# A hybrid decoder layer on one core: the second half's second FFN product in four accumulation steps, two of them by block products

## The chip, the cores and the metric

The program runs on one core of a Trainium2 chip. Times are device microseconds of one execution (us). The core's engines are TensorE (PE in the profile, its weight loads PEld), VectorE (DVE), ScalarE (ACT), GpSimd (POOL) and SyncE (SP). Each executes its own list of instructions in order. Transfers are issued by SyncE, GpSimd and (at the very end) ScalarE, and carried by 16 transfer engines that they share.

## What is computed

One layer, weights shared by a prompt (1 x 1024 tokens) and a sample group (8 x 4 tokens), model width 1024, FFN width 2816:

```python
h = _rmsnorm(x, norm1_g) * (1.0 + sc1) + sh1       # sh, sc, gt from silu(c) @ ada_w + ada_b
u = h @ w_in                                       # inputs of both branches and of the gates
y_a = h_lru * gelu(u_g)                            # causal convolution, RG-LRU
y_b = o * silu(u_r)                                # chunked GLA, head norm
m = sigmoid(u_ga) * (y_a @ proj_a) + sigmoid(u_gb) * (y_b @ proj_b)
x = x + gt1 * (m @ w_out)
h2 = _rmsnorm(x, norm2_g) * (1.0 + sc2) + sh2
f1, f2 = jnp.split(h2 @ ffn_w1, 2, axis=-1)
x = x + gt2 * ((silu(f1) * f2) @ ffn_w2)
y = _rmsnorm(x, final_g)
```

Everything is float32.

## The kernel before

The tokens are worked through in two halves, one after the other: half A has 512 prompt tokens, half B the other 512 and the 32 sample tokens (544). Activations lie with features on the partitions and tokens in the columns. A product is made of tiles of 128 x 128 weights against all tokens of a half. For precision each float32 operand is split in a high and a low part (ScalarE copies the high part, VectorE subtracts: `split_w` at L147 for weights, L150 and L151; `split` for activations), and a tile costs three matmuls (L407 to L409): high x high, high x low, low x high. Half B has two pieces of 272 columns, so a tile of it costs six matmuls.

A half runs `branches` (projections, RG-LRU, GLA, then `merge_b` and `merge_a`) and `back` (output projection, second norm, FFN). The FFN has 22 feature tiles: a gate and an up column each, called a couple here. Its first product is made for couples 0 to 10, then the second product adds these eleven to x (`ffn2`, L1356), then couples 11 to 21 and the second product again.

Couples 6 to 21 go by block products in `ffn1_fast` (L1277): gate and up column, the two halves of the input features and the two halves of the tokens form a 2 x 2 x 2 block product that needs seven products instead of eight (a Winograd form), with four input tiles each, 84 matmuls instead of 96 at half B's width. It needs sums and differences of blocks of the weights and of the activations. `weight_sums` (L344) makes those of the weights once, during half A: it loads two tiles on SyncE's queue, makes four VectorE operations and stores both results in the DRAM tile `wsum` on GpSimd's queue. It is a generator that is moved on in half A's merges. `block_sums` (L1245) makes those of the activations, beside the first four couples (`ffn1_first`, by token halves) and couples 4 and 5 (`ffn1`).

A scheduler sets the order on each engine when the program is built. It takes what is ready, the earlier written first; the code's order is a priority and no bound. The PE list inside `ffn1_fast` alone is held as written (`as_written`), and copies under `tc.high_priority(AHEAD)` come earlier. Buffers come from pools of a fixed number by tag: five raw weight tiles, three split ones (`hl`), six of tag `t`, seventeen of tag `S`.

The start of the program is `begin` (L518). It loads x and the modulation weights (`ada`), takes the norm's sum of squares (`acc1a`, L442), the reciprocal root (`rsqrt`, L302 to L309, last row `rstd1a`), scales the inputs (`xn1a`, L515), splits the low-rank weights (`lr_hla`, L586) and works four early projections (`early`, split at L151) by parts as the inputs come.

## Time and profile before

| | |
|---|---|
| timed runs | 1987.34, 1992.32, 1989.97 us; median 1989.97 |
| profiled execution | 1986.12 us, its span 1984.3 us |
| granted TensorE clock, mean | 0.995 |
| TensorE, VectorE, ScalarE, GpSimd busy | 98%, 63%, 46%, 4% of the span |
| bytes moved | 287 MB, mean 145 GB/s |
| x of half B is loaded | from 900.2 us |
| half B's first `ffn1_fast` matmul, last matmul of the second product | 1672.5, 1973.7 us |

In a list of groups a row is: line, engine, operation, output<-input, shapes, count | busy us, mean ns of one | idle time of the engine just before, and what ended it. In a timeline a row is: start, duration, engine, line, operation, and in brackets the idle time before it. In a table of stretches a row is: the stretch, its length, then busy us and count of PE, PEld, DVE, ACT, POOL, then the granted clock, the share of the transfer engines and GB/s. A wait's row has the total, the number and the longest. The issue list has the count, the size and the median us from issue to landing.

### The profile page before, as it was taken

Reading aid. Unit: us, or ns where it says so; the run is one execution under the profiler, and the core shown is the slowest. Engines: PE = TensorE matmul, PEld = TensorE weight load, DVE = VectorE, ACT = ScalarE, POOL = GpSimd, SP = SyncE. Lnnn points to the kernel's source line nnn. Section 1 sums busy time; section 2 is a strip of 40 time slices with the busy share of each in tenths; the row PEclk is TensorE's granted clock in tenths of the full one; section 3 lists DMA queues with packets and bytes.
Section 4 is the critical chain, followed back from the end, with each engine's and each line's share of the span. In section 5 each row is a group of like instructions: output and inputs, shape, how many; then the busy total and the mean of one; then the engine's idle time right before and its main releaser. Section 6 shows DMA issues by size and latency. Waiting matters only on the chain. (4 is left out here: it accounts for less than half of the span.)

```text
span 1984.3 us, 33357 instructions
## 1 busy us (share of the span) xinstructions
PE 1947.3 (98%) x13524; PEld 1771.8 (89%) x13524; DVE 1252.6 (63%) x2126; ACT 913.9 (46%) x1377; POOL 77.8 (4%) x159
## 2 busy tenths in 40 slices
PE   8999999999999999999999999999999999999998
PEld 5877877777789998998899999899999999999997
DVE  5648487665558763677564597784243597636776
ACT  3645475533235452555353355563332354415553
POOL 0000021000000000000000001010000000000000
PEclk9999999999999999999999999999999999999999
DMA  8334236567764453554422313323223434435553
GB/s 337 103 99 165 70 138 212 194 239 262 250 212 155 137 156 114 174 180 137 153 90 84 116 62 107 106 86 106 70 89 107 159 126 138 137 104 170 172 156 117
DMA packets 106906, 287.34 MB, mean 145 GB/s; under 512 B 12288, under 2 KB 20224, under 8 KB 106752
## 3 DMA queue, kind: packets, MB, share of 16 engines
q1 hardware_dynamic: 98608, 257.20, 40.0%
q0 software_dynamic: 7600, 27.45, 3.7%
q8 instruction: 106, 1.74, 0.3%
q10 hardware_dynamic: 544, 0.56, 0.1%
q14 instruction: 48, 0.39, 0.1%
HBM read 259.16 MB, written 26.01 MB: 144 GB/s over the span
## 5 line engine op out<-in xcount | busy, mean ns | idle before, releaser
L151 DVE TENSOR_TENSOR fwa_hl<-fwa,fwa_hl 128x1024 fp32r<-128x1024 f32 (+1 forms) x57 | 68.8, 1207 | 44.6 <-ACT fwa_hl L150 40.8
L151 DVE TENSOR_TENSOR fwb_hl<-fwb,fwb_hl 128x1024 fp32r<-128x1024 f32 (+1 forms) x57 | 68.8, 1206 | 40.0 <-ACT fwb_hl L150 36.1
L150 ACT ACTIVATE fwa_hl<-fwa 128x1024 fp32r<-128x1024 f32 (+1 forms) x57 | 59.3, 1039 | 44.0 <-PE fapsa L1305 10.8
L150 ACT ACTIVATE fwb_hl<-fwb 128x1024 fp32r<-128x1024 f32 (+1 forms) x57 | 59.3, 1040 | 33.3 <-PE fcpsb L1305 8.0
L150 ACT ACTIVATE f3b_hl<-f3b_raw 128x768 fp32r<-128x768 f32 (+1 forms) x45 | 35.7, 794 | 74.5 <-PE f3psb L409 21.4
L407 PE MATMUL f3psa<-faa,f3a_hl 128*128 128x512 f32 x176 | 68.6, 390 | 0.6 <-ACT f3a_hl L150 0.6
L409 PE MATMUL f3psa<-faa,f3a_hl 128*128 128x512 f32 x176 | 68.5, 390 | 0.4 <-DVE f3a_hl L151 0.4
L408 PE MATMUL f3psa<-faa,f3a_hl 128*128 128x512 f32 x176 | 68.6, 390 | 0.0
L151 DVE TENSOR_TENSOR f3b_hl<-f3b_raw,f3b_hl 128x768 fp32r<-128x768 f32 (+1 forms) x45 | 40.2, 893 | 35.7 <-ACT f3b_hl L150 34.6
L150 ACT ACTIVATE f3a_hl<-f3a_raw 128x768 fp32r<-128x768 f32 (+1 forms) x32 | 25.3, 792 | 56.6 <-PE f3psa L409 48.1
L409 PE MATMUL f3psb<-fab,f3b_hl 128*128 128x272 f32 x176 | 50.6, 288 | 0.0
L408 PE MATMUL f3psb<-fab,f3b_hl 128*128 128x272 f32 x176 | 50.5, 287 | 0.0
L407 PE MATMUL f3psb<-fab,f3b_hl 128*128 128x272 f32 x176 | 50.5, 288 | 0.0
L407 PE MATMUL uxpsb<-h1b,uxpsb_hl 128*128 128x256 f32 (+1 forms) x160 | 47.3, 296 | 0.1
L408 PE MATMUL uxpsb<-h1b,uxpsb_hl 128*128 128x256 f32 (+1 forms) x160 | 46.3, 290 | 0.0
L151 DVE TENSOR_TENSOR f3a_hl<-f3a_raw,f3a_hl 128x768 fp32r<-128x768 f32 (+1 forms) x32 | 28.5, 890 | 28.2 <-ACT f3a_hl L150 24.6
L407 PE MATMUL ugpsb<-h1b,ugpsb_hl 128*128 128x272 f32 x160 | 46.3, 289 | 0.0
L409 PE MATMUL ugpsb<-h1b,ugpsb_hl 128*128 128x272 f32 x160 | 46.1, 288 | 0.0
L409 PE MATMUL uxpsb<-h1b,uxpsb_hl 128*128 128x256 f32 (+1 forms) x160 | 46.0, 288 | 0.0
L408 PE MATMUL ugpsb<-h1b,ugpsb_hl 128*128 128x272 f32 x160 | 45.9, 287 | 0.0
L407 PEld LDWEIGHTS f3psa<-faa,f3a_hl 128*128 128x128 f32 x176 | 33.0, 188 | 7.7 <-ACT f3a_hl L150 1.0
L409 PEld LDWEIGHTS f3psa<-faa,f3a_hl 128*128 128x128 f32 x176 | 33.0, 188 | 7.7 <-DVE f3a_hl L151 0.9
(1132 smaller groups left out, 7616.8 us busy)
## 6 DMA issues: line engine op xcount, KB each, us to landing
ada<-in_ada_w SPq DMA_DIRECT2D x48, 512.0 KB, 6.4
s_raw<-in_ffn SPq DMA_DIRECT2D x32, 512.0 KB, 3.9
wsum<-s_raw POOLq DMA_DIRECT2D x32, 512.0 KB, 3.7
fwa<-wsum SPq DMA_DIRECT2D x64, 256.0 KB, 3.4
fwb<-wsum SPq DMA_DIRECT2D x64, 256.0 KB, 3.4
fwa<-in_ffn SPq DMA_DIRECT2D x48, 256.0 KB, 3.3
fwb<-in_ffn SPq DMA_DIRECT2D x48, 256.0 KB, 3.3
f3b_raw<-in_ffn SPq DMA_DIRECT2D x23, 384.0 KB, 3.1
```

Of the source, the lines that this page charges most:

```text
L150: act.activation(hl[:, 0, :n], raw[:, :n], AF.Copy)
L151: dve.tensor_sub(hl[:, 1, :n], raw[:, :n], hl[:, 0, :n].bitcast(F32))
L407: pe.matmul(out, wh, x[:, o:o + w], start=st, stop=False)
L408: pe.matmul(out, wh, x[:, N + o:N + o + w], start=False, stop=False)
L409: pe.matmul(out, wl, x[:, o:o + w], start=False, stop=en)
```

## The change

Only half B's FFN is computed in another way; half A's couples, sums and second product stay.

- Couples 4 and 5 of half B go by blocks too. Beside its block sums stand, instead of them, features 0 to 3 of the second product.
- Half B's second product is added to x in four steps: features 0 to 3 directly, 4 to 9 and 10 to 15 by the new `ffn2_fast`, 16 to 21 directly by token halves. In `ffn2_fast` two output tiles, two groups of three features and the two token halves form the blocks: seven products of three tiles, 63 matmuls for a pair of output tiles, where the direct way takes 72. Features are sorted for that (`KF`).
- `keep` makes the sums of a couple's results that `ffn2_fast` reads, in place of one split per feature.
- `late_sums` makes the weights' sums for all this: four jobs for couples 4 and 5 (two of 256 columns for each), eight for the second product (384 columns). A job loads two tiles on GpSimd's queue, makes four VectorE operations and stores both on GpSimd's queue. It has two buffers of its own (tag `sums`). The code moves it on in half B's merges.
- `dynamic_dma_scratch_size` goes from 8192 to 4096.

```diff
-FAST = 6
+FAST = (6, 4)
+KF = (3, 2, 1, 0, 4, 6, 8, 5, 7, 9, 10, 12, 14, 11, 13, 15, 16, 17, 18, 19, 20, 21)
...
+    wsum2 = {(q, g): drp.tile([P, 1536], F32, name=f"wsumf{q}{g}") for q in range(4) for g in range(2)}
...
+    def late_sums():
+        jobs = []
+        halves = lambda t, u, c: t.rearrange("p (n u) -> p n u", n=2)[:, :, c * u:(c + 1) * u]
+        for f in range(FAST[1], FAST[0]):
+            for c in range(2):
+                to = [halves(wsum[f][:, v * 1024:(v + 1) * 1024], 256, c) for v in range(2)]
+                jobs.append((256, [halves(I["ffn1"][2 * f + v], 256, c) for v in range(2)], to))
+        for g in range(2):
+            for q in range(4):
+                c = P * (4 + 6 * g)
+                to = [halves(wsum2[q, g][:, v * 768:(v + 1) * 768], 384, 0) for v in range(2)]
+                jobs.append((384, [halves(I["ffn2"][2 * q + v][:, c:c + 768], 384, 0) for v in range(2)], to))
+        for k, (u, src, to) in enumerate(jobs):
+            r = [wp.tile([P, 768], F32, tag="sums", name=f"sums{k}{v}", bufs=2) for v in range(2)]
+            rv = [t[:, :2 * u].rearrange("p (n u) -> p n u", n=2) for t in r]
+            for v in range(2):
+                pool.dma_start(rv[v], src[v])
+            yield 1
+            r1, r2 = rv
+            dve.tensor_add(r2[:, 1], r2[:, 0], r2[:, 1])
+            dve.tensor_sub(r2[:, 0], r1[:, 0], r2[:, 0])
+            dve.tensor_sub(r1[:, 0], r2[:, 1], r1[:, 0])
+            dve.tensor_sub(r1[:, 1], r1[:, 1], r1[:, 0])
+            for v in range(2):
+                pool.dma_start(to[v], rv[v])
+            yield 1
...
                 if s.hf == 0:
                     next(sums_of, None)
+                elif j >= 4:
+                    next(sums_late, None)
+                    next(sums_late, None)
...
+                if s.hf:
+                    next(sums_late, None)
...
-                if s.hf == 0:
-                    next(sums_of, None)
+                next(sums_late if s.hf else sums_of, None)
...
+        def keep(s, f, tg):
+            N, W = s.N, s.N // 2
+            if not (s.hf and 4 <= f < 16):
+                a = s.act[f] = S(f"fa{s.n}{f}", F32R)
+                split(a, tg[:, :N], N)
+                return
+            p, odd = divmod(f - 4, 2)
+            hi, lo, nn = slice(0, W), slice(W, N), slice(0, N)
+            if not odd:
+                o = p % 2 * W
+                if o == 0:
+                    s.b11 = S(f"f11{p}", F32R)
+                h, l = s.b11[:, o:o + W], s.b11[:, N + o:N + o + W]
+                act.activation(h, tg[:, lo], AF.Copy)
+                dve.tensor_sub(l, tg[:, lo], h.bitcast(F32))
+                dve.tensor_sub(tg[:, lo], tg[:, hi], tg[:, lo])
+                s.even = tg
+                s.fs["11"].append((h, l))
+                return
+            ta, tb = s.even, T(f"fb{s.n}{f}")
+            dve.tensor_sub(tb[:, hi], tg[:, hi], ta[:, lo])
+            dve.tensor_sub(tb[:, lo], tg[:, lo], tb[:, hi])
+            dve.tensor_sub(ta[:, hi], tg[:, hi], ta[:, hi])
+            for c, src, part, whole in ("y", tb, "t4", "t2"), ("x", tg, "21", "22"), ("z", ta, "t1", "t3"):
+                t = S(f"f{c}{s.n}{f}", F32R)
+                split(t, src[:, nn], N)
...
+        def ffn2_fast(s, g):
...
+            for q in range(4):
+                pa, pb, pc = [mm(f"g{c}ps{n}")[:, 0, :W] for c in "abc"]
+                v1, v2 = T("ga" + n), T("gb" + n)
+                product(pa, "11", True)
+                s.snap(v1[:, lo], pa)
+                product(pb, "t1", True)
+                s.snap(v2[:, lo], pb)
+                product(pa, "t2", False)
+                s.snap(v1[:, hi], pa)
+                product(pb, "22", False)
+                product(pa, "t3", False)
+                s.snap(v2[:, hi], pa)
+                dve.tensor_add(v1[:, hi], v1[:, hi], pb)
+                product(pc, "21", True)
+                dve.tensor_add(v1[:, lo], v1[:, lo], pc)
+                dve.tensor_add(v2[:, hi], v2[:, hi], v2[:, lo])
+                onto(2 * q, v1)
+                product(pa, "t4", False)
+                act.activation(v2[:, lo], pa, AF.Copy)
+                onto(2 * q + 1, v2)
...
+            mix(chain(s.ffn1_first(p1, EARLY), s.ffn2(0, 4, s.whole)), b)
+            drain(b)
+            drain(s.ffn1_fast(range(4, 11)))
+            drain(s.ffn2_fast(0))
+            drain(s.ffn1_fast(range(11, 17)))
+            drain(s.ffn2_fast(1))
+            s.keep(16, s.late)
...
-    drain(B.ffn1_fast(range(11, NF)))
+    drain(B.ffn1_fast(range(17, NF)))
...
-    drain(B.ffn2(1, p1, a1))
-    dn = B.ffn2(1, p0, a0)
+    drain(B.ffn2(16, NF, p1, a1))
+    dn = B.ffn2(16, NF, p0, a0)
```

Where the scheduler put the jobs of `late_sums` is seen in the lists. In these rows `sums` with a number is a buffer of a job, `wsum` and `wsumf` are the DRAM tiles; in brackets stand the semaphores that a row waits for, DMASW being transfers of GpSimd and DMAHW those of SyncE.

GpSimd at the start of the program, before:

```order
L126 MEMSET rmask 128x576
L130 MEMSET hist 128x30
L127 MEMSET rmask 128x4 [waits Pool_49]
L128 MEMSET rmask 128x16
L274 DMA wa2raw<-in_wa 128x512 [waits DMAHW4_49,PE_49]
L1018 COPY uba_1854<-hist 128x3 [waits PE_49,DVE_49,Activation_49,Pool_49]
```

and now:

```order
L130 MEMSET hist 128x30
L373 DMA sums_13288<-in_ffn 128x2x256
L127 MEMSET rmask 128x4 [waits Pool_49]
L128 MEMSET rmask 128x16
L373 DMA sums_13289<-in_ffn 128x2x256
L381 DMA wsum_78<-sums_13289 128x2x256 [waits DMASW2_49,DVE_49]
L381 DMA wsum_78<-sums_13288 128x2x256 [waits DMASW1_49,DVE_49]
L373 DMA sums_13410<-in_ffn 128x2x256 [waits DMASW3_49]
L373 DMA sums_13411<-in_ffn 128x2x256 [waits DMASW4_49]
```

The other eleven jobs follow in the same way, `wa2raw` in the midst of the seventh, and all of them stand ahead of the first `uba`. A job's loads wait for the stores of the job before.

VectorE at the end of the first reciprocal root, before:

```order
L307 TENSOR_TENSOR rs_1a<-rs_1a,ri_1a 128x4 [waits DVE_49]
L309 SCALAR_TENSOR_TENSOR rs_1a<-rs_1a,ri_1a 128x4 [waits DVE_49]
L306 SCALAR_TENSOR_TENSOR rs_1a<-rs_1a 128x4 [waits DVE_49]
L307 TENSOR_TENSOR rs_1a<-rs_1a 128x4 [waits DVE_49]
L309 SCALAR_TENSOR_TENSOR rstd1a<-rs_1a 128x4 [waits DVE_49]
L221 TENSOR_REDUCE mod<-adat_264 128x36 [waits PE_49]
```

and now:

```order
L307 TENSOR_TENSOR rs_1a<-rs_1a 128x4 [waits DVE_49]
L376 TENSOR_TENSOR sums_13411<-sums_13411 128x256 [waits DMASW6_49,DMASW4_49]
L309 SCALAR_TENSOR_TENSOR rstd1a<-rs_1a 128x4 [waits DVE_49]
L295 TENSOR_SCALAR sp_140<-lw 128x10
L377 TENSOR_TENSOR sums_13411<-sums_13410,sums_13411 128x256 [waits DMASW5_49,DVE_49]
L378 TENSOR_TENSOR sums_13410<-sums_13411,sums_13410 128x256 [waits DMASW3_49,DVE_49]
L379 TENSOR_TENSOR sums_13410<-sums_13410 128x256 [waits DVE_49]
L221 TENSOR_REDUCE mod<-adat_274 128x36 [waits PE_49]
```

The second job (job 1) stands around `rstd1a`, its first addition one row ahead of it.

VectorE between the scaled inputs and `lr_hla`, before:

```order
L515 SCALAR_TENSOR_TENSOR xn1a_272<-xa_144,gains,rb1a 128x512 [waits DMAHW2_49,DVE_49,Activation_49]
L515 SCALAR_TENSOR_TENSOR xn1a_274<-xa_144,gains,rb1a 128x512
L515 SCALAR_TENSOR_TENSOR xn1a_276<-xa_146,gains,rb1a 128x512 [waits DMAHW3_49]
L515 SCALAR_TENSOR_TENSOR xn1a_278<-xa_146,gains,rb1a 128x512
L586 TENSOR_TENSOR lr_hla<-lr_raw,lr_hla 128x8x16 [waits DMAHW6_49,DMAHW2_49,Activation_49]
```

and now, from the row after the last of the four:

```order
L376 TENSOR_TENSOR sums_13533<-sums_13533 128x256 [waits DMASW2_49,DMASW0_49]
L377 TENSOR_TENSOR sums_13533<-sums_13532,sums_13533 128x256 [waits DMASW1_49,DVE_49]
L378 TENSOR_TENSOR sums_13532<-sums_13533,sums_13532 128x256 [waits DMASW7_49,DVE_49]
L379 TENSOR_TENSOR sums_13532<-sums_13532 128x256 [waits DVE_49]
L376 TENSOR_TENSOR sums_13655<-sums_13655 128x256 [waits DMASW6_49,DMASW4_49,DVE_49]
L377 TENSOR_TENSOR sums_13655<-sums_13654,sums_13655 128x256 [waits DMASW5_49,DVE_49]
L378 TENSOR_TENSOR sums_13654<-sums_13655,sums_13654 128x256 [waits DMASW3_49,DVE_49]
L379 TENSOR_TENSOR sums_13654<-sums_13654 128x256 [waits DVE_49]
L376 TENSOR_TENSOR sums_13722<-sums_13722 128x384 [waits DMASW2_49,DMASW0_49,DVE_49]
L377 TENSOR_TENSOR sums_13722<-sums_13721,sums_13722 128x384 [waits DMASW1_49,DVE_49]
L378 TENSOR_TENSOR sums_13721<-sums_13722,sums_13721 128x384 [waits DMASW7_49,DVE_49]
L614 TENSOR_TENSOR lr_hla<-lr_raw,lr_hla 128x8x16 [waits DMAHW6_49,DMAHW2_49,Activation_49]
```

Jobs 2, 3 and 4 now stand between them. Jobs 5 and 6 follow two splits of `early_hl` later, ahead of the third.

More of the change, by code (lines that the diff above doesn't have):

```diff
@@ L76, in hybrid_layer @@
     drp = ctx.enter_context(tc.tile_pool(name="drp", bufs=1, space=bass.MemoryType.DRAM))
-    wsum = {f: drp.tile([P, 2048], F32, name=f"wsum{f}") for f in range(FAST, NF)}
+    wsum = {f: drp.tile([P, 2048], F32, name=f"wsum{f}") for f in range(FAST[1], NF)}
+    wsum2 = {(q, g): drp.tile([P, 1536], F32, name=f"wsumf{q}{g}") for q in range(4) for g in range(2)}
     def S(name, dt=F32):
@@ L344, in weight_sums @@
     def weight_sums():
-        for f in range(FAST, NF):
+        for f in range(FAST[0], NF):
             r1, r2 = load_raw(I["ffn1"][2 * f], 1024, f"s1{f}"), load_raw(I["ffn1"][2 * f + 1], 1024, f"s2{f}")
@@ L1275, in block_sums, with products, weights, product @@
                 yield 10
+        def products(s, units, u, of, name):
+            now = [0, None]
+            def weights():
+                k = now[0]
+                now[0] += 1
+                if k % 2 == 0:
+                    raw = wp.tile([P, 1024], F32, tag="raw", name=f"{name}{k}", bufs=5)
+                    two = units[k:k + 2]
+                    for j, src in enumerate(two):
+                        sp.dma_start(raw[:, j * u:(j + 1) * u], src)
+                    now[1] = split_w(raw, u * len(two), f"{name}{k}")
+                return now[1], k % 2 * u
+            def product(out, key, first):
+                hl, c = weights()
+                for i, (xh, xl) in enumerate(of[key]):
+                    wh, wl = hl[:, 0, c + i * P:c + (i + 1) * P], hl[:, 1, c + i * P:c + (i + 1) * P]
+                    pe.matmul(out, wh, xh, start=first and i == 0, stop=False, skip_group_check=True)
+                    pe.matmul(out, wh, xl, start=False, stop=False, skip_group_check=True)
+                    pe.matmul(out, wl, xh, start=False, stop=i == len(of[key]) - 1, skip_group_check=True)
+            return product
```

111 lines of the change are left out of this document (56 added, 55 removed).

## The prediction

> **What bounds the kernel now.** I read the engines' totals first, then TensorE's waits, then the busy time by stretches.
>
> ```profile
> span 1984.3 us, 33357 instructions
> PE 1947.3 (98%) x13524; PEld 1771.8 (89%) x13524; DVE 1252.6 (63%) x2126; ACT 913.9 (46%) x1377; POOL 77.8 (4%) x159
> ```
>
> ```profile
> PE gapsa L409 <- DVE gapsa_hl L151: 4.4, 1, 4.4
> PE adaps L208 <- DMA ada<-in_ada_w: 1.2, 1, 1.2
> ```
>
> ```profile
> 0.00:50.00 50.00, 44.71 (x264) 27.36 (x265) 28.85 (x83) 19.79 (x31) 2.32 (x12) 0.97 0.87 334
> ...
> 1720.00:1740.00 20.00, 20.00 (x163) 20.00 (x162) 9.81 (x18) 6.36 (x9) 0.00 (x0) 1.00 0.37 110
> 1860.00:1880.00 20.00, 20.00 (x162) 20.00 (x161) 13.96 (x21) 11.85 (x19) 0.00 (x0) 1.00 0.58 175
> ```
>
> TensorE is the bound: busy 98% of the span, and its longest single wait is 4.4 us. So a matmul that goes away shortens the span, and a stall put ahead of TensorE's work lengthens it by the same amount, since nothing behind has slack to take it back. The price of one matmul of 272 columns is read from the stretches, not from the duration in a group: 163 start in 20 us, so one costs **0.123 us** (a record lists 0.288 us because neighbours overlap). In the block stage (1860 to 1880) VectorE is busy 13.96 of 20 us.
>
> The one part of the kernel where TensorE isn't the bound is the start, which waits for weights:
>
> ```profile
> DMA  1999999999999999981000637300007421508609
> GB/s 28 243 385 383 418 419 413 410 410 405 400 411 406 410 395 390 398 320 43 0 0 0 210 43 256 128 0 3 0 0 210 111 98 18 198 13 336 280 0 277
> ada<-in_ada_w SPq DMA_DIRECT2D x19, 512.0 KB, 10.8
> wa2raw<-in_wa POOLq DMA_DIRECT2D x1, 256.0 KB, 6.6
> ```
>
> These are the transfers of the first 100 us in slices of 2.5 us: from 2.5 to 45 us the transfer engines are full at about 405 GB/s. In that time SyncE's 512 KB take 10.8 us to land, and the one transfer that GpSimd issues into the backlog (256 KB) takes 6.6.
>
> **The change part by part.**
>
> *Matmuls.* A couple by blocks takes 7 products x 4 tiles x 3 = 84 matmuls where the direct way takes 96; two couples save 24. Twelve features of the second product take 8 x 63 = 504 instead of 8 x 72 = 576; that saves 72. The orders agree: 12192 rows on TensorE, now 12096. 96 x 0.123 = **-11.8 us**, all on the path.
>
> *Sums of weights.* Twelve jobs are added (4 of 256 KB halves, 8 of 384 KB). Each loads two tiles on GpSimd's queue, makes four VectorE operations that depend on each other, and stores both. The code hands them out in the second half's merges, but the orders on GpSimd and VectorE (shown with the change) put all twelve at the very start of the program: nothing they need is computed, so they were moved up. There they have one pair of buffers, so job k+1 can't load before job k's stores have landed; and VectorE executes in order, so everything queued behind a job's first addition waits for that load. GpSimd reaches the first load around the memsets of rmask and needs 0.55 us for an issue. The VectorE rows that get stuck are those of the first norm and the first projections:
>
> ```profile
> 2.72 0.12 POOL L128 MEMSET rmask<- 128x16 f32 x1
> 21.66 0.55 POOL L274 DMA_DIRECT2D wa2raw<-in_wa  x1 [18.81 <-PE adaps L208]
> ```
>
> ```profile
> 11.85 0.68 DVE L442 TENSOR_TENSOR acc1a<-acc1a,sq1a 128x512 f32<-128x512 f32 x1
> 16.55 0.16 DVE L309 SCALAR_TENSOR_TENSOR rstd1a<-rs_1a 128x4 f32<-128x4 f32 x1
> 23.23 0.29 DVE L586 TENSOR_TENSOR lr_hla<-lr_raw,lr_hla 128x128 fp32r<-128x128 f32 x1
> 38.68 1.23 DVE L151 TENSOR_TENSOR early_hl<-early_raw,early_hl 128x1024 fp32r<-128x1024 f32 x1 [7.62 <-ACT early_hl L150]
> 50.49 0.69 DVE L607 TENSOR_TENSOR lrta<-lrpsa,lrta 16x512 fp32r<-16x512 f32 x1 [1.44 <-ACT lrta L605]
> ...
> 93.58 0.77 DVE L822 COPY_PREDICATED atta<-lmask,spsa 128x256 f32<-128x256 int32 x2 [3.55 <-PE spsa L805]
> 110.87 1.31 DVE L822 COPY_PREDICATED atta<-lmask,spsa 128x256 f32<-128x256 int32 x2 [5.51 <-PE spsa L805]
> ```
>
> The price of one turn, from landings and VectorE's durations (first all transfers of the tile wsum, GpSimd's 32 stores among them; then 256 KB and 384 KB loads on SyncE; then operations by width, those of the 256-wide half A and the 272-wide half B):
>
> ```profile
> DMA to landing us min/median/max: 2.9/3.4/6.9
> fwb<-in_ffn SPq DMA_DIRECT2D x48, 256.0 KB, 3.3
> f3b_raw<-in_ffn SPq DMA_DIRECT2D x23, 384.0 KB, 3.1
> ```
>
> ```profile
> L1333 DVE TENSOR_TENSOR fta<-fta,vba 128x256 f32<-128x256 f32 x16 | 6.8, 426 | 0.6
> L1327 DVE TENSOR_TENSOR vab<-vab,fbpsb 128x272 f32<-128x272 f32 x16 | 6.9, 432 | 2.5 <-PE fbpsb L1305 2.5
> L1337 DVE TENSOR_TENSOR fab<-ftb,fab 128x544 fp32r<-128x544 f32 x16 | 11.5, 719 | 0.0
> ```
>
> Four dependent additions cost 4 x 0.45 = 1.8 us at 256 wide and, by the line through the 272 and 544 rows, about 4 x 0.59 = 2.35 at 384 (0.03 between two of them). A transfer on GpSimd's queue isn't in the trace at this place and in this shape (1 KB pieces), so I bound it: 2.9 us below (the fastest landing of wsum), 10.8 above (SyncE's median in the backlog). I take 6.6 while the backlog lasts, GpSimd's own row in it, and 3.4 after. The backlog ends near 41 us again: SyncE can have 14 MB out before it needs a buffer that VectorE holds, two jobs add 2 MB, and 16.2 MB / 405 GB/s = 40 us from 2.5.
>
> The chain then, job by job (0 to 11):
> - Job 0 issues its second load at 3.4 and lands at 10.0. The norm's six additions queue behind it and end near 16.5 in place of 12.5. Its second store goes out at 12.6 and lands at 19.2.
> - Job 1 loads 19.2 to 25.8. Its first addition stands one row ahead of the last of the reciprocal root, so rstd1a comes at 26.3 in place of 16.55: +9.7.
> - Jobs 2, 3 and 4 stand between the scaled inputs and lr_hla. Loads land at 27.6 + 6.6 + 6.6 = 40.8; then 40.8 + 1.8 + 3.4 + 3.4 = 49.4; then 57.9. lr_hla starts at 59.7 in place of 23.23: **+36.5**.
> - Jobs 5 and 6 stand ahead of the third split of early_hl. Job 5 lands at 67.2, where VectorE arrives at 67.4; job 6 lands at 76.4. The split starts at 77.0 in place of 38.68: +38.3. Three more of its additions stand within the next rows, 1.7 us, so that lrta is about 40 us late.
> - Jobs 7 to 11 are spread over work that has gaps (VectorE waits 3.55 and 5.51 us ahead of the last two rows); jobs 10 and 11 come about 10 us apart against a turn of 9, so I add 1.
>
> Sum at the start: **+41 us**. By the fastest landing throughout, the same chain has turns of 7.65 and 8.15 us: lr_hla at 40.2 (+17), the third split at 56, sum +19.5. By 10.8 in the first three jobs and 3.4 after, lr_hla comes at 77 (+54), sum +60. I take the middle case because it is the only one with a GpSimd transfer in the same backlog. At 50 us TensorE's queue is behind by that much, and with 98% busy afterwards nothing is given back; SyncE's prefetch gains from the pause, but only the 1.2 us wait above could shrink.
>
> The Trainium skill (DMA: Bandwidth & Descriptors, "Anatomy of one DMA" and "Queues, rings and completion order") gives a transfer on this path as 2.0 us plus bytes over 436 GB/s, and lets each transfer engine alternate between queues, so that GpSimd wouldn't stand behind SyncE's backlog. By it a 256 KB load costs 2.6 us (estimate) and the start would come out near +18. For the wsum stores of 512 KB it gives 3.2 and the trace 3.4; for wa2raw in the backlog it gives 2.6 and the trace 6.6, so here the trace speaks against it.
>
> *Second half, block stage.* The direct pairs beside the block sums (192 matmuls) become ffn2 over four features (also 192): nothing. Every product still reads kept or prefetched weights. New VectorE work per couple of even and odd feature is 3 x 0.72 + 5 x 0.43 - 2 x 0.72 = 2.9 us; an average couple has 13.96/20 of 10.3 = 7.2, so an odd one reaches about 10 us. A step of the second product has 63 x 0.123 = 7.7 us of TensorE and on VectorE 3.5 splits, three additions and the two residuals:
>
> ```profile
> L151 DVE TENSOR_TENSOR f3b_hl<-f3b_raw,f3b_hl 128x768 fp32r<-128x768 f32 x8 | 7.7, 958 | 0.8 <-ACT f3b_hl L150 0.4
> L1309 ACT ACTIVATE vab<-fapsb 128x272 f32<-128x272 f32 x31 | 12.2, 394 | 16.0 <-PE fapsb L1305 15.7
> ```
>
> 3.5 x 0.96 + 3 x 0.43 + 2 x 1.1 = 6.9 us, under 7.7. A snapshot (0.394 us on ScalarE) must end within one product, now 9 x 0.123 = 1.1 us instead of 1.5, with a 0.85 us split at times ahead of it. So it is covered, but closely. Below: 0. Above: each of six odd couples waits for its three splits, 6 x 2.2 = 13 us. Three split weight buffers hold two products each, 5.9 us ahead of TensorE in the first product and 4.4 in the second, which is nearer to 0; I take **+3**, the shorter last stage (18 matmuls, 2.2 us a tile, against 4.1) included.
>
> Sum: 1986.1 - 11.8 + 41 + 3 = 2018. The profiled execution lies 3.9 us under the median of the runs shown (1989.97); a timed median may lie that much above the sum, and I carry over 1 us of it: **2019 us**.
>
> **The rivals.**
> - *Short transfers.* GpSimd's loads land in 2.9 us even in the backlog: +19.5, and 1986.1 - 11.8 + 19.5 + 1 = 1995. For it: the fastest wsum landings; against it wa2raw. The Trainium skill's rule above (DMA: Bandwidth & Descriptors) leads to about the same. Chance 0.12.
> - *Long transfers.* The 1 KB pieces fare as SyncE's in the backlog: +60, 2038. For it: full engines until 45 us; against it, again wa2raw. Chance 0.10.
> - *The blocks don't pay.* VectorE at 10 of 10.3 us in odd couples stops TensorE and gives back the 11.8: 13 in place of 3, 2029. Against it: no wait of the block stage is among TensorE's waits before. Chance 0.10.
> - *Faster.* The jobs land before VectorE reaches their rows, and only the matmuls count: 1986.1 - 11.8 + 3 = 1977. It decides at job 4, which must land by 23.2 us; with job 0 at 6.3 that leaves (23.2 - 6.3)/4 = 4.2 us a turn, and the shortest turn of the rows is 7.65. Only two landings and the additions make 2.9 + 1.8 + 2.9. Chance 0.04.
>
> **How the numbers follow.** 0.64 stays for the forecast, with its own range 2005 to 2030. A change under 0.3% (6 us) can't be told from none by this measurement. The faster case gives 0.04; the upper part of 1984 to 1996 takes two thirds of the short transfers, 0.08; the rest, 0.88, is slower. For 8 in 10 the range starts in the short transfers at 1997 and ends at the long ones, 2038.
>
> **What would show it.** Right: VectorE's longest waits all before 130 us, on transfers of in_ffn into sums; lr_hla near 60 us; TensorE's busy share of the first 50 us well under the 44.7 of now; from the third projection on the same pace as before, and the block stages about 12 us shorter. Wrong: lr_hla before 35 us, landings of sums at 3 us in the first 40; or waits of TensorE on fvb_hl, or on VectorE's copies of the features, of over 5 us in total.

## The result and the profile after

The changed kernel takes **2053.46 us** (median of 5 runs, 2049.41 to 2057.85) against 1992.32 (5 runs, 1987.34 to 1992.69) before: a ratio of 1.0306, 95% interval 1.0284 to 1.0329. It is slower, as forecast, but by 61 us where 29 were forecast, and 15 us above 2038, the upper end of the wider of the two ranges (8 in 10). The profiled execution took 2049.41 us.

The engines' totals, and the shares of TensorE and its granted clock in 40 slices of the span (51.2 us each):

```profile
span 2047.6 us, 33637 instructions
PE 1950.7 (95%) x13428; PEld 1770.0 (86%) x13428; DVE 1319.9 (64%) x2293; ACT 943.2 (46%) x1442; POOL 106.4 (5%) x207
...
PE   4698999999999999999999999999999999999998
...
PEclk8799999999999999999999999999999999999999
```

96 matmuls fewer, as counted, and still a longer span: TensorE's share falls from 98% to 95%, and the loss lies in the first slices. TensorE's longest waits, and VectorE's on the new loads (total, times, longest):

```profile
PE lrpsa L620 <- ACT h1a L514: 29.7, 2, 28.6
PE spsa L833 <- DVE atta L850: 7.5, 1, 7.5
PE nps1a L442 <- DVE acc1a L470: 5.1, 1, 5.1
...
PE fapsb L1328 <- ACT vab L1336: 4.0, 3, 1.5
PE vtpa L684 <- DVE atta L754: 3.8, 1, 3.8
```

```profile
DVE sums L376 <- DMA sums<-in_ffn: 62.6, 11, 9.5
```

Eleven of the twelve jobs made VectorE stand still, 62.6 us in all. What stood behind each first addition (L376) is seen in VectorE's timeline:

```profile
11.72 0.42 DVE L376 TENSOR_TENSOR sums<-sums 128x256 f32<-128x256 f32 x1 [6.57 <-DMA sums<-in_ffn]
...
27.71 0.43 DVE L376 TENSOR_TENSOR sums<-sums 128x256 f32<-128x256 f32 x1 [4.34 <-DMA sums<-in_ffn]
28.05 0.15 DVE L309 SCALAR_TENSOR_TENSOR rstd1a<-rs_1a 128x4 f32<-128x4 f32 x1
...
44.20 0.42 DVE L376 TENSOR_TENSOR sums<-sums 128x256 f32<-128x256 f32 x1 [9.55 <-DMA sums<-in_ffn]
...
62.30 0.56 DVE L376 TENSOR_TENSOR sums<-sums 128x384 f32<-128x384 f32 x1 [7.72 <-DMA sums<-in_ffn]
...
63.96 0.28 DVE L614 TENSOR_TENSOR lr_hla<-lr_raw,lr_hla 128x128 fp32r<-128x128 f32 x1
...
82.83 0.56 DVE L376 TENSOR_TENSOR sums<-sums 128x384 f32<-128x384 f32 x1 [7.41 <-DMA sums<-in_ffn]
83.30 1.22 DVE L151 TENSOR_TENSOR early_hl<-early_raw,early_hl 128x1024 fp32r<-128x1024 f32 x1
...
92.26 0.69 DVE L276 TENSOR_TENSOR wa<-wa2raw,wa 16x512 fp32r<-16x512 f32 x1 [2.35 <-ACT wa L275]
...
98.12 0.69 DVE L635 TENSOR_TENSOR lrta<-lrpsa,lrta 16x512 fp32r<-16x512 f32 x1 [1.42 <-ACT lrta L633]
...
132.63 0.55 DVE L376 TENSOR_TENSOR sums<-sums 128x384 f32<-128x384 f32 x1
...
150.62 0.56 DVE L376 TENSOR_TENSOR sums<-sums 128x384 f32<-128x384 f32 x1 [7.62 <-DMA sums<-in_ffn]
...
162.70 0.56 DVE L376 TENSOR_TENSOR sums<-sums 128x384 f32<-128x384 f32 x1 [3.06 <-DMA sums<-in_ffn]
```

The place is the one that the prediction named, row for row; two things differ. The chain is longer at each job (lr_hla at 63.96, not 59.7), and the jobs from 8 on, which were costed at next to nothing, go on blocking until 163 us. There TensorE loses again (20 us stretches; busy us of PE, PEld, DVE, ACT, POOL, then the granted clock):

```profile
40.00:60.00 20.00, 0.00 (x0) 0.00 (x0) 3.40 (x8) 0.00 (x0) 5.41 (x8) 0.55 0.61 212
...
120.00:140.00 20.00, 16.16 (x113) 12.96 (x113) 18.37 (x26) 10.67 (x16) 2.17 (x4) 0.91 0.47 155
140.00:160.00 20.00, 16.33 (x94) 12.22 (x92) 11.35 (x18) 9.32 (x16) 3.27 (x6) 1.00 0.65 241
160.00:180.00 20.00, 15.34 (x78) 12.16 (x78) 8.27 (x14) 4.01 (x7) 1.09 (x2) 0.83 0.51 176
```

The delay against the kernel before, read at the same instructions of the two traces (first or last start of an operation, us):

| instruction | before | later by | since the row above |
|---|---|---|---|
| lr_hla | 23.2 | 40.8 | +40.8 |
| lrta | 50.5 | 47.6 | +6.8 |
| last matmul into kpsa | 115.9 | 63.5 | +15.9 |
| last matmul into f1psa (first half's FFN) | 661.0 | 65.7 | +2.2 |
| last matmul into f1psb (second half's FFN) | 1645.1 | 68.0 | +2.3 |
| first matmul into fapsb (block stage) | 1672.5 | 68.7 | +0.7 |
| last matmul into f3psb | 1973.6 | 62.6 | -6.1 |

So 47.6 us at the start (forecast: 40), 15.9 in the stage of values and keys (forecast: 1), 4.5 in the merges and after (forecast: nothing), and -5.4 in the second half's FFN (forecast: -8.8).

### The profile page after: what moved, and what is told of

Same layout as the page of the kernel before. It is cut to its first block, busy times and chain, and to the rows that moved or that the text cites. A ratio compares the mean times of both kernels' runs of the same rounds, so it can differ in the third digit from the quotient of the medians.

```text
span 2047.6 us, 33637 instructions
## 1 busy us (share of the span) xinstructions
PE 1950.7 (95%) x13428; PEld 1770.0 (86%) x13428; DVE 1319.9 (64%) x2293; ACT 943.2 (46%) x1442; POOL 106.4 (5%) x207
## 5 line engine op out<-in xcount | busy, mean ns | idle before, releaser
L151 DVE TENSOR_TENSOR fwa_hl<-fwa,fwa_hl 128x1024 fp32r<-128x1024 f32 (+1 forms) x57 | 68.8, 1207 | 44.6 <-ACT fwa_hl L150 40.5
L151 DVE TENSOR_TENSOR fwb_hl<-fwb,fwb_hl 128x1024 fp32r<-128x1024 f32 (+1 forms) x64 | 77.2, 1206 | 29.6 <-ACT fwb_hl L150 29.1
L150 ACT ACTIVATE fwb_hl<-fwb 128x1024 fp32r<-128x1024 f32 (+1 forms) x64 | 66.7, 1042 | 34.2 <-issue 10.7
L150 ACT ACTIVATE fwa_hl<-fwa 128x1024 fp32r<-128x1024 f32 (+1 forms) x57 | 59.2, 1039 | 44.0 <-PE fapsa L1330 10.8
L436 PE MATMUL f3psa<-faa,f3a_hl 128*128 128x512 f32 x176 | 68.7, 390 | 0.0
L435 PE MATMUL uxpsb<-h1b,uxpsb_hl 128*128 128x256 f32 (+1 forms) x160 | 47.9, 299 | 0.1
L376 DVE TENSOR_TENSOR sums<-sums 128x384 f32<-128x384 f32 (+1 forms) x12 | 6.2, 513 | 62.6 <-DMA sums<-in_ffn 62.6
L435 PEld LDWEIGHTS f3psa<-faa,f3a_hl 128*128 128x128 f32 x176 | 33.1, 188 | 7.7 <-ACT f3a_hl L150 1.0
L437 PEld LDWEIGHTS f3psa<-faa,f3a_hl 128*128 128x128 f32 x176 | 33.0, 188 | 7.6 <-DVE f3a_hl L151 0.9
L348 DVE TENSOR_TENSOR s_raw<-s_raw 128x512 f32<-128x512 f32 x16 | 11.0, 690 | 44.3 <-DMA s_raw<-in_ffn 44.3
L436 PEld LDWEIGHTS f3psa<-faa,f3a_hl 128*128 128x128 f32 x176 | 33.1, 188 | 6.8
L435 PE MATMUL rpsb<-h1b,rpsb_hl 128*128 128x272 f32 x128 | 37.8, 295 | 0.0
L435 PE MATMUL wopsb<-mb,wob_hl 128*128 128x272 f32 x128 | 36.8, 288 | 0.9 <-DVE gab L1198 0.9
```

The lines of the kernel that those rows point to most:

```text
L150: act.activation(hl[:, 0, :n], raw[:, :n], AF.Copy)
L151: dve.tensor_sub(hl[:, 1, :n], raw[:, :n], hl[:, 0, :n].bitcast(F32))
L348: dve.tensor_add(r2[:, 512:1024], r2[:, 0:512], r2[:, 512:1024])
L376: dve.tensor_add(r2[:, 1], r2[:, 0], r2[:, 1])
L435: pe.matmul(out, wh, x[:, o:o + w], start=st, stop=False)
L436: pe.matmul(out, wh, x[:, N + o:N + o + w], start=False, stop=False)
```

## The experiments

The theory to be tested: the loss is VectorE standing, in order, at additions whose load isn't there; the FFN itself is faster. The rivals: the new transfers (8 MB loaded and 8 MB stored; the expectations say 9 MB, which is wrong) slow the weights, and VectorE's wait only shows it; or part of the loss lies in the new FFN. Each kernel has line numbers of its own. The comparisons name the median of the kernel before on the same chip.

**The jobs alone, with the old FFN.** The kernel before with `late_sums` and its calls, the scratch for GpSimd's transfers as in the change:

```diff
+    sums_of, sums_late = weight_sums(), late_sums()
...
-                if s.hf == 0:
-                    next(sums_of, None)
+                next(sums_late if s.hf else sums_of, None)
```

> The kernel before with the twelve jobs alone (their sums are stored and not used), which its scheduler puts at the same rows of the program's start; FFN as before, the smaller scratch for GpSimd's transfers as in the changed kernel. Theory (the start is the whole loss): before + 63 us, 2050 to 2060 us, lr_hla at 64. Rival 2 (part of the loss lies in the new FFN): before + 55 or less.

Measured: 2055.39 us (4 runs, 2053.65 to 2057.44) against 1991.94, ratio 1.0319 (1.0304 to 1.0335). The same jobs with none of the new arithmetic cost 63 us. In VectorE's timeline:

```profile
64.22 0.28 DVE L615 TENSOR_TENSOR lr_hla<-lr_raw,lr_hla 128x128 fp32r<-128x128 f32 x1
...
101.41 0.69 DVE L636 TENSOR_TENSOR lrta<-lrpsa,lrta 16x512 fp32r<-16x512 f32 x1 [3.02 <-ACT lrta L634]
```

lr_hla is 41.0 us late, lrta 50.9. The jobs alone give the whole loss. The two intervals overlap, so the times don't show what the rest of the change brings; the traces do: from the first matmul into fapsb to the last into f3psb the delay is unchanged here and falls by 6.1 us in the changed kernel.

**The transfers without the additions.** The four VectorE operations of each job are left out, and wa2raw goes ahead of the jobs:

```diff
-            r1, r2 = rv
-            dve.tensor_add(r2[:, 1], r2[:, 0], r2[:, 1])
-            dve.tensor_sub(r2[:, 0], r1[:, 0], r2[:, 0])
-            dve.tensor_sub(r1[:, 0], r2[:, 1], r1[:, 0])
-            dve.tensor_sub(r1[:, 1], r1[:, 1], r1[:, 0])
```

> The changed kernel without the four VectorE additions of each job: the twelve jobs' loads and stores stay at the program's start, and the stores write the loaded weights as they are, so the block products are fed unsummed weights; wa2raw is issued ahead of the jobs so that it does not stand behind them on GpSimd. Theory (VectorE's queue): with nothing of the jobs on VectorE, lr_hla starts within 5 us of 23.2 and the run takes 1988 to 1997 us. Rival 1 (traffic): the transfers alone slow the weights, lr_hla starts after 45 us, the run takes 2030 us or more.

Measured: 1993.39 us (10 runs, 1989.93 to 1999.02) against 1991.94, ratio 1.0006 (0.9994 to 1.0019). VectorE's rows:

```profile
27.98 0.29 DVE L609 TENSOR_TENSOR lr_hla<-lr_raw,lr_hla 128x128 fp32r<-128x128 f32 x1 [2.58 <-ACT lr_hla L608]
...
59.05 0.69 DVE L630 TENSOR_TENSOR lrta<-lrpsa,lrta 16x512 fp32r<-16x512 f32 x1 [2.59 <-ACT lrta L628]
```

The same bytes at the same place cost 4.8 us at lr_hla and 8.6 at lrta, and no more up to the last vpsa; another 4.4 us come by the last wopsa (the table below), for a cause that stays open. The jobs' additions, and not the traffic, are the cause of about 39 of the 47.6 us. Of these, less than 2 belong to wa2raw, which this run moves too (the run wa2first); the rest is the wait in VectorE's queue. The transfers follow each other faster here, so 8.6 is rather too much for their share.

**Jobs 8 to 11 elsewhere.** Each job's first load is held behind the GpSimd row written before it and its first addition behind the VectorE row written before it, for k from 8 on:

```diff
+                if v == 0 and k >= 8:
+                    in_place(mybir.EngineType.Pool)
...
+            if k >= 8:
+                in_place(mybir.EngineType.DVE)
```

> Jobs 0 to 7 at the start as in the changed kernel; jobs 8 to 11 kept in the second half's merges. Theory (jobs 8 to 11 block VectorE between 110 and 163 us): lr_hla at 64 and lrta at 98 as in the changed kernel, the last vpsa 216.7 - 15.9 = 201 us, the run 2038 us (2034 to 2043). Rival (the loss between 100 and 217 us follows from how the start ended: late prefetch, a lower granted clock): the last vpsa at 212 or later, the run 2049 or more.

Measured: 2039.51 us (4 runs, 2039.12 to 2040.16) against 1991.94, ratio 1.0240 (1.0224 to 1.0255): 14 us under the changed kernel. lr_hla and lrta are as late as in it (40.5 and 47.9), and the last vpsa starts 47.9 us late instead of 63.4, at 201.6. The stretches have no gap any more:

```profile
120.00:140.00 20.00, 19.70 (x137) 15.99 (x136) 15.28 (x21) 12.30 (x20) 0.00 (x0) 1.00 0.37 112
140.00:160.00 20.00, 20.00 (x124) 15.34 (x123) 11.74 (x21) 10.28 (x14) 0.00 (x0) 1.00 0.50 178
160.00:180.00 20.00, 20.00 (x111) 16.33 (x110) 6.53 (x10) 3.09 (x4) 0.00 (x0) 1.00 0.33 106
```

The 15.9 us are jobs 8 to 11 and nothing that the start leaves behind, neither a late prefetch nor the lower clock of the start.

**wa2raw ahead of the jobs.** The small load that GpSimd issues for the gate's weights stood behind six jobs and the first store of the seventh. Of the changed kernel, the tile's rows and ScalarE's wait for it:

```profile
L274 POOL DMA_DIRECT2D wa2raw<-in_wa x1: 537/537/537, 86.4 to 86.4; - x1
```

```profile
ACT wa L275 <- DMA wa2raw<-in_wa: 11.0, 1, 11.0
```

```diff
+    wraw = S("wa2raw")
+    pool.dma_start(wraw[:, :NH * P].rearrange("p (h m) -> p h m", m=P), I["wa2"])
...
-        wraw = S("wa2raw")
...
-        pool.dma_start(w3, I["wa2"])
```

> The changed kernel, with wa2raw issued from GpSimd ahead of the jobs instead of behind seven of them. Theory (a second queue: wa2raw was issued at 86.4 us in place of 21.7, and VectorE waited 2.35 us for what ScalarE makes of it): lrta about 2.4 us earlier (45 us late instead of 47.6), the run 2051 us. Rival (wa2raw is hidden): lrta as in the changed kernel.

Measured: 2050.02 us (4 runs, 2045.19 to 2053.93) against 1994.19, ratio 1.0289 (1.0271 to 1.0307). lrta starts at 96.42, 1.7 us earlier than in the changed kernel. The ratio's interval overlaps the changed kernel's, so the time says nothing; the trace shows a second queue with the same fault, and its price at lrta is near 2 us (2.4 were expected). By the last kpsa this execution is 3.6 us earlier; whether the rest of that is wa2raw wasn't tested.

**The jobs where the code hands them out.** All twelve are held in the second half's merges, as jobs 8 to 11 above.

> The twelve jobs of sums are kept where the code hands them out, in the second half's merges: each job's first load stands behind the GpSimd row written before it, its first addition behind the VectorE row written before it. Nothing else changes. Theory (VectorE's queue at the start): the +47.6 us up to lrta and the +15.9 us more up to the end of the values stage go away whole, and what stays is the second FFN product (-5.3 us measured between the kernels) and the small shifts: 1985 to 1990 us against 1992.3 before. Rival 1 (the traffic of the jobs, 9 MB in all, wherever it lies): the same bytes now take the place of the merges' weights, TensorE waits there, 2005 us or more. Rival 2 (the second FFN product itself costs): 1993 or more, with waits of TensorE after the merges.

Measured: 2010.28 us (4 runs, 2009.77 to 2014.61) against 1991.94, ratio 1.0097 (1.0081 to 1.0114). The theory's number was wrong, rival 1's was right, but not its mechanism. The start is as before (lr_hla 0.7 us earlier), and the second half's merges lose 23.8 us (papsb: first matmul 3.6 us late, last 27.4):

```profile
DVE sums L384 <- DMA sums<-in_ffn: 60.6, 12, 7.7
```

VectorE waits for the loads there just as at the start, 60.6 us for twelve jobs: GpSimd reaches the first load only at 1447.9, behind copies of `tails` that wait for VectorE, and with one pair of buffers each later load goes out after the stores of the job ahead. TensorE waits for the splits queued behind (13.6 us on gapsb_hl alone). Putting work "where there is time" isn't enough; its load must be out well before.

**The jobs in the first half's FFN, three steps apart.** The loads go out two steps ahead of the additions:

```diff
+    def with_sums(g):
+        for w in g:
+            if turn[0] % 3 != 1:
+                next(sums_late, None)
+            turn[0] += 1
+            yield w
...
+    drain(with_sums(A.ffn1_fast(range(11, NF))))
```

> The twelve jobs are handed out in the first half's FFN (block stages and second product, one job per three steps of some 5 to 8 us, the loads two steps ahead of the additions), and kept there as in the run late; the merges of the second half are as before. Theory (what a job costs is the time that VectorE stands at its first addition ahead of work that TensorE needs): with the load landed before VectorE arrives, nothing is lost, and only the second half's FFN is left, -5.4 us: 1987 us (1984 to 1990), no wait of VectorE on sums over 1 us. Rival (any place costs, since VectorE or the transfers have no room beside block products): TensorE waits appear in the first half's FFN, 1995 us or more.

Measured: 2004.62 us (6 runs, 1997.17 to 2010.52) against 1994.19, ratio 1.0052 (1.0034 to 1.0070): neither number. VectorE's wait on sums fell from 62.6 to:

```profile
DVE sums L384 <- DMA sums<-in_ffn: 16.7, 4, 5.9
```

Four jobs, 11 to 15 us behind the one ahead, still waited; of the other eight, the first has none ahead, seven stand 17 us and more behind, and none waited. In stretches of 10 us TensorE loses time next to a job that waited (its addition starts at 820.23, after 4.40 us of waiting) and none next to one that did not (844.66):

```profile
820.00:830.00 10.00, 7.55 (x50) 7.56 (x51) 7.91 (x13) 3.47 (x7) 1.63 (x3) 0.83 0.62 183
...
840.00:850.00 10.00, 10.00 (x86) 10.00 (x85) 9.35 (x15) 5.03 (x9) 1.43 (x3) 1.00 0.68 197
```

From the last f1psa to the last f3psa the first half's FFN loses 17.3 us. That is more than VectorE's 16.7 us of waiting, so the waits are not the whole of it; the run apart, below, shows what is left without them.

**The second half's FFN by itself.** Two kernels beside the last one. In the first, a split copy of weights on ScalarE may not stand ahead of a snapshot that can be taken before it; this moves three copies:

```diff
+                    old = [i for p, i in s.snaps if p <= k - 6]
+                    if old:
+                        copy = [i for i in list(traced())[begin:] if i.engine == mybir.EngineType.Activation][0]
+                        tc.add_manual_dep(copy, old[-1].name, after, reason="snap first")
```

> As the run spread, but a split copy of weights on ScalarE may not stand ahead of a snapshot that can be taken before it. This moves three copies, those behind the three waits of TensorE on ScalarE's snapshot (4.0 us) in the first block stage of the second half. Theory (these copies wait for a buffer that TensorE frees only after the snapshot's bank is free): 3 to 4 us under spread. Rival (the wait has another cause, VectorE or the feature splits): within 1 us of spread.

In the second, the two middle accumulation steps are direct:

```diff
-            drain(s.ffn2_fast(0))
+            drain(s.ffn2(4, 10, s.whole))
...
-            drain(s.ffn2_fast(1))
+            drain(s.ffn2(10, 16, s.whole))
```

> As the run spread, but the two middle accumulation steps of the second product are done directly (six features each, 72 matmuls more), and no feature is split for blocks; only the two more gate/up couples by blocks remain of the change's arithmetic. Theory (72 x 0.123 = 8.9 us, less 4.0 us of snapshot waits and about 1 us that the second product's feature work costs): 4 us over spread, and no wait of TensorE on snapshots. Rival (the waits have nothing to do with the second product's features): 9 us over spread, snapshot waits as in it.

Measured: snapfirst 2002.06 us (6 runs, 2000.53 to 2005.98), couples 2010.33 (5 runs, 2008.44 to 2013.37), spread 2004.62, all against 1994.19. The first half scatters by several us between these executions, so I read the second half's FFN in the traces, from the first matmul into fapsb to the last into f3psb, against the kernel before: **-6.1 us** in spread, **-10.6** with the copies behind the snapshots, **-2.9** with the second product direct. The waits of TensorE on snapshots of fapsb (4.0 us, three times, in the changed kernel and in spread) are gone in both. So the first theory holds (4.5 us, 3 to 4 expected); the second's loss against spread is 3.2 us in these traces, 4 expected, and its rival's 9 us with waits is out. The matmuls count for 11.8 us of which 10.6 arrive once that order is mended; the two more couples alone bring 2.9 of their 3.0. One of the three waits in the changed kernel, and a stretch of the second product:

```profile
1760.00:1780.00 20.00, 18.52 (x148) 18.30 (x148) 15.71 (x25) 11.81 (x20) 0.00 (x0) 1.00 0.51 159
...
1840.00:1860.00 20.00, 20.00 (x163) 20.00 (x162) 15.62 (x28) 11.60 (x19) 0.00 (x0) 1.00 0.69 214
```

VectorE, at 15.7 of 20, isn't the bound; the second product's own stage (1840 to 1860) runs full.

**The additions on GpSimd, in the first half.** All twelve jobs one behind the other from the end of the first half's merges, without and with the order of the copies from snapfirst:

```diff
-            dve.tensor_add(r2[:, 1], r2[:, 0], r2[:, 1])
+            pool.tensor_add(r2[:, 1], r2[:, 0], r2[:, 1])
...
+    drain(sums_late)
     A.act = {}
```

> The changed kernel with the four additions of each job on GpSimd instead of VectorE, all twelve jobs one behind the other from the end of the first half's merges on, where GpSimd has no other work; same loads and stores, VectorE has nothing of the jobs. Theory (a job costs only where VectorE stands at it): nothing of the start, the values stage or the first half's FFN is lost; the second half's FFN brings -5.4 us: 1988 us (1985 to 1991), no TensorE wait in the first half's FFN that the kernel before does not have. Rival (VectorE's additions or the 9 MB beside the block stage cost of themselves): 1995 us or more, TensorE waits between 560 and 970 us.

> As the run poolsums, with the three split copies on ScalarE behind the snapshots as in the run snapfirst. Theory (the three waits come of that order): 4 us under poolsums, 1984 us, and so 0.4% under the kernel before. Rival (what snapfirst showed was chance): as poolsums.

Measured: 2011.04 us (6 runs, 2001.21 to 2014.97) and 2006.11 (6 runs, 1996.69 to 2013.69) against 1994.12; ratios 1.0077 (1.0051 to 1.0103) and 1.0062 (1.0038 to 1.0085). The theory's numbers are missed by some 20 us. VectorE has nothing of the jobs now, and yet it is full in stretches between the second norm and the block sums, and TensorE starves. In the kernel before, VectorE was busy 15 to 20 of every 20 us there (600 to 680). Of poolsums:

```profile
660.00:680.00 20.00, 17.18 (x123) 16.17 (x122) 19.96 (x35) 9.72 (x19) 9.39 (x12) 0.91 0.59 204
680.00:700.00 20.00, 17.46 (x116) 15.89 (x115) 20.00 (x31) 9.80 (x17) 11.24 (x12) 1.00 0.65 218
```

Its own operations have grown longer. Groups of VectorE between 600 and 720 us, of poolsums and then of the kernel before:

```profile
L509 DVE SCALAR_TENSOR_TENSOR xn2a<-xma,gains,rb2a 128x256 f32<-128x256 f32 x16 | 10.1, 676 | 0.5 <-ACT rb2a L465 0.5
...
L1278 DVE TENSOR_TENSOR faa<-fta,faa 128x256 fp32r<-128x256 f32 x8 | 5.8, 722 | 0.0
...
L1229 DVE SCALAR_TENSOR_TENSOR xma<-wopsa,gains,xra 128x256 f32<-128x256 f32 x8 | 3.8, 478 | 6.3 <-DMA xra<-in_xa 6.3
```

```profile
L473 DVE SCALAR_TENSOR_TENSOR xn2a<-xma,gains,rb2a 128x256 f32<-128x256 f32 x16 | 6.9, 478 | 0.0
...
L1242 DVE TENSOR_TENSOR faa<-fta,faa 128x256 fp32r<-128x256 f32 x8 | 3.3, 416 | 0.0
...
L1193 DVE SCALAR_TENSOR_TENSOR xma<-wopsa,gains,xra 128x256 f32<-128x256 f32 x6 | 2.9, 483 | 3.3 <-DMA xra<-in_xa 2.5 <-PE wopsa L409 0.8
```

Operations with two large inputs in SBUF take 676 for 478 ns and 722 for 416 on average. Most of them take what they took before (medians 473 and 416 ns), and a few are longer by about one GpSimd addition (longest 1617 and 1241 ns). Those that read a product from PSUM stay as they were (from wopsa 478 for 483, from f1psa 408 for 412). The Trainium skill (SBUF — State Buffer, "Who interferes with whom") says that a VectorE instruction with two SBUF inputs can't overlap a GpSimd instruction that reads SBUF, and that the later one waits for the whole of the other; these rows agree with it. That this is the whole of the loss isn't shown: the jobs' transfers run there too (VectorE waits 6.3 us for the loads of xra, 2.5 before), and 9.1 us are lost by the last wopsa already. Whether poolsnap's copies brought their 4 us can't be told from times that scatter by 17 us; the traces do tell it, since from the first fapsb to the last f3psb poolsums gains 6.1 us and poolsnap 10.6.

**Two kernels in which no job should cost.** The first is snapfirst with the jobs four steps apart, one ahead of the block stage and one behind it:

```diff
-            if turn[0] % 3 != 1:
+            if turn[0] % 4 < 2:
                 next(sums_late, None)
```

> As the run snapfirst (VectorE's additions in the first half's FFN, copies behind snapshots), but the jobs stand four steps apart instead of three, one ahead of the block stage and one behind it, so that the next load is out some 10 us before VectorE arrives. Theory (a job costs what VectorE waits for its load, and nothing where the load has landed): no VectorE wait on sums over 1 us, the first half's FFN as before, and the second half's FFN brings 9 to 10 us: 1983 us (1980 to 1987) against 1992 to 1994 before. Rival (12 x 2.2 us of VectorE's work or 9 MB beside the block products cost of themselves, as poolsums might be read): 1992 us or more, with TensorE waits in the first half's FFN and none of VectorE's on sums.

The second is poolsnap with its jobs in the second half's merges, eight from the third step of `merge_b` on and four behind the copies of `tails`:

```diff
+                elif j == 2:
+                    for _ in range(16):
+                        next(sums_late)
...
                 pool.dma_start(O["tails"], tails)
+                drain(sums_late)
```

> As the run poolsnap (additions on GpSimd, copies behind snapshots), but the jobs lie in the second half's merges, where VectorE is busy 39 of 100 us, instead of the first half's normalisation, where it is busy 20 of 20. Theory (GpSimd's additions lengthen VectorE's operations beside them, 416 to 722 ns for the additions of faa, which costs only where VectorE is the bound): no loss in the first half, at most 3 us in the merges, 1984 to 1988 us. Rival (GpSimd's additions or the transfers cost TensorE anywhere): 1995 us or more, waits of TensorE on splits in the second half's merges.

Measured: apart 1989.63 us (11 runs, 1984.77 to 1993.20) against 1992.57, ratio **0.9979** (0.9966 to 0.9992); poolmerge 1985.33 (6 runs, 1977.92 to 1986.01), ratio **0.9969** (0.9957 to 0.9981). Both lie a little below the kernel before, by 0.2% and 0.3%, with intervals that leave out 1; apart's 0.2% is under the 0.3% that the prediction took for the limit of this measurement. poolmerge, of the same arithmetic as the changed kernel, is 68 us faster than that. Its profiled execution (1977.92 us) is the fastest of its six, as that of the kernel before (1986.12) is faster than all its timed runs; by medians the gain is 7.2 us. Its span and the engines' busy time:

```profile
span 1976.1 us, 33596 instructions
...
PE 1937.1 (98%) x13428; PEld 1760.8 (89%) x13428; DVE 1308.5 (66%) x2245; ACT 943.4 (48%) x1442; POOL 159.8 (8%) x255
```

In poolmerge the delay is 0.8 us at the end of the first half's output projection, 1.0 at the second half's last pbpsb, 2.1 at the first fapsb and -8.6 at the last f3psb: the block stages and the second product bring 10.7 us again, and the jobs cost nothing measurable. Between 1300 and 1560 us TensorE has no wait over 0.9 us, though VectorE's operations are longer beside GpSimd's there as well (from 1300 to 1400 us it is busy 58.2 us, 53.1 before); it has room. In apart VectorE no longer waits on sums at all, and the second half's FFN brings 10.6 us, but 6.7 us are lost by the end of the first half's output projection and 6.6 more by the end of its FFN (3.7 of it one wait of TensorE on f3a_hl), so the expected 1983 was missed. So a job whose load has landed is cheaper than one that waits, and not shown to be free: on VectorE it still adds work to a stage that uses 43 of 60 us. A loss ahead of the FFN, by the end of the output projection, comes back in these kernels in several sizes (0.8 us in poolmerge, 11.6 in poolsnap); which part of it is the first loads, issued at 558 to 560 us, and which is chance wasn't settled.

The points of the traces behind these readings, as delays in us against the kernel before:

| instruction | before | sums_alone | traffic | hold8 | late | spread | poolsums | apart | poolmerge |
|---|---|---|---|---|---|---|---|---|---|
| lrta | 50.5 | 50.9 | 8.6 | 47.9 | -0.2 | 1.3 | -0.1 | -0.2 | 0.4 |
| last vpsa | 153.7 | 66.2 | 8.5 | 47.9 | -0.2 | 1.4 | -0.1 | -0.3 | 0.4 |
| last wopsa | 614.0 | 67.8 | 13.0 | 52.8 | 1.6 | 4.0 | 9.1 | 6.7 | 0.8 |
| last f3psa | 970.1 | 67.8 | 12.6 | 53.1 | 2.1 | 21.3 | 29.2 | 13.3 | 1.0 |
| last pbpsb | 1436.8 | 67.2 | 12.5 | 55.1 | 3.6 | 22.9 | 30.9 | 13.2 | 1.0 |
| first fapsb | 1672.5 | 67.5 | 13.5 | 58.2 | 29.0 | 23.7 | 32.0 | 13.9 | 2.1 |
| last f3psb | 1973.6 | 67.5 | 7.5 | 52.1 | 22.9 | 17.6 | 26.0 | 3.3 | -8.6 |

## Why the prediction was right and wrong

**Right: the bound, the mechanism, the place.** The hoisted jobs block VectorE in order, and TensorE waits behind: sums_alone has the whole loss without the new FFN, and traffic, with all the bytes and without the additions, has 8.6 of the 47.6 us at lrta. TensorE is busy 25.4 us of the first 50 (44.7 before), the FFN has 96 matmuls fewer, and no wait of TensorE on fvb_hl or the features' copies appears.

**The step that failed: "jobs 7 to 11 are spread over work that has gaps ... so I add 1".** It measured +15.9 us, nearly half of the 31 us between the sum's 2018 and the profiled 2049. Two errors stand in it. The turn was worked out as 9 us from landings and additions alone. The real turns of these jobs are 12 to 18 us (100.33, 114.24, 132.63, 150.62, 162.70), since a job's operations stand between other VectorE rows and GpSimd waits for each of them. GpSimd's rows between the additions of 132.63 and 150.62, in the changed kernel:

```profile
138.18 0.55 POOL L381 DMA_DIRECT2D wsumf<-sums  x1 [0.64 <-DVE sums L379]
141.05 0.55 POOL L373 DMA_DIRECT2D sums<-in_ffn  x1 [2.33 <-DMA wsumf<-sums]
143.45 0.54 POOL L373 DMA_DIRECT2D sums<-in_ffn  x1 [1.85 <-DMA wsumf<-sums]
```

5.6 us to the second store, 5.3 from there to the second load, 7.2 until it is used: 18. And VectorE's gaps ahead of atta (3.55 and 5.51 us) were taken as room. They were waits for TensorE's own spsa, whose next step needs atta at once; a wait put there delays TensorE whole, as its 7.5 us on atta show. hold8 shows the price of the two errors together, not the share of each: with the four jobs gone the stage loses nothing. TensorE's two waits for atta (3.8 and 7.5 us) are 11.3 of the 15.9 us. Behind each it is busy throughout and at a lower granted clock (0.75 from 125 to 130 us, 0.65 from 165 to 170); as an estimate, 5 x 0.25 + 5 x 0.35 = 3 us more are lost by that, a term that the prediction doesn't have.

**Mis-sized: the start, 40 forecast and 47.6 measured.** The chain was right, and the landing prices were near. Loads and stores of 256 KB up to 44 us, while the transfer engines are full, and from 44 to 56 us (size, median us from issue to landing):

```profile
sums<-in_ffn POOLq DMA_DIRECT2D x6, 256.0 KB, 6.5
wsum<-sums POOLq DMA_DIRECT2D x4, 256.0 KB, 6.4
```

```profile
wsum<-sums POOLq DMA_DIRECT2D x4, 256.0 KB, 2.7
sums<-in_ffn POOLq DMA_DIRECT2D x2, 256.0 KB, 3.2
```

The sum took 6.6 and then 3.4 for both. But the slowest landing of a turn counts (8.3 us for job 0's second load, 7.8 for job 1's second store, 5.1 for job 5's second load), an issue of the 256 KB loads keeps GpSimd 0.71 us, not 0.55, and the waits between add to each turn: job 0 came 1.7 us late, job 2 3.4, job 4 4.4, job 6 6.4. The last 1 to 2 us are a term that wasn't in the sum at all: wa2raw, whose row at 21.66 the prediction quotes, now stood in the midst of the seventh job on GpSimd. It was used as a price and not as an instruction that is moved past. By the rule from the Trainium skill (DMA: Bandwidth & Descriptors, "Anatomy of one DMA"), 2.6 us for such a load, the start would have been +18 (an estimate). The 6.5 us measured while the transfer engines are full are against it, as wa2raw was before; the 2.7 and 3.2 us behind the backlog are near it. The 3.4 that the prediction sets beside this rule for stores of 512 KB is the median of all transfers of the tile wsum; the stores alone took 3.7.

**Mis-sized: the FFN, -11.8 and +3 forecast, -11.8 and +6.4 measured.** Snapshots were named as covered "but closely". They weren't in the first block stage: 4.0 us, by three copies of weights that stand ahead of them on ScalarE. In the changed kernel the first of them starts at 1765.44 us, 0.08 us after TensorE's last matmul ahead of its wait has ended; that fits a copy that waits for a buffer of weights TensorE still reads, though the profile names no releaser. snapfirst puts them behind the snapshots and the stage with its second product comes to -10.6. What the prediction feared more, VectorE at 10 of 10.3 us, did not come: 15.7 of 20. The +6.4 is what is left of -5.4 when the matmuls are taken at -11.8; snapshots explain 4.5 of it, the rest isn't placed.

**Not forecast at all: +4.5 us** in the first half's merges and the second half's RG-LRU stage. In sums_alone 1.6 us of it appear in the first half and nothing in the second. It changes from kernel to kernel, and its cause is open.

**The rivals.** Short transfers are out (medians of 6.5 and 6.4 us at the start); their sum, 1995, also leaves out the +3 of the FFN that the other sums have, and is 1998 with it. Long ones (10.8) are out too, though the time came near their 2038 and past it by other terms. "The blocks don't pay" was half true (-5.4 us of -11.8) and for another reason than VectorE. The faster case failed where it was said to be decided: job 4's first addition starts at 62.3, not by 23.2. The list of signs had one that proved false at once and could have been looked for: VectorE's waits on sums went on to 163 us.

## What to carry to other kernels

Work with no inputs of its own is moved to the front by a scheduler that takes what is ready, and its price isn't its duration but how long an in-order engine stands at it: place the load a full turn ahead (in the first half's FFN, with one pair of buffers, jobs 17 us and more behind the one before didn't wait), and hold the addition where it is written. Work out a turn from every row that it passes on both engines, not from the landings alone, and list all that is queued behind on the engine that issues (here wa2raw). A gap on an engine is only room if nobody waits for what follows it: VectorE's waits for TensorE in a tight exchange were not.
